# A hybrid decoder trunk on one core: the residual is updated before it is multiplied by the next norm's weights

## The chip, the core and the metric

One Trainium2 chip, of which the kernel uses one core. Its engines are PE (TensorE, matmuls; PEld is its weight load), DVE (VectorE), ACT (ScalarE), POOL (GpSimd) and SP (which here only issues transfers). They run side by side and meet through semaphores. The metric is the device time of one execution in microseconds (us); less is better.

## The reference, cut to what matters

Two layers over 256 tokens of width 1024. Each layer has two "sandwich" norms: the output of a block is normalised and added to the residual x, and x is normalised again before the next block.

```python
def _rms_norm(x, g):
    y = x * rsqrt(mean(x * x, axis=-1) + 1e-6)
    return y * g
...
for l in range(DEPTH):
    h = _rms_norm(x, g_pre_mix[l])
    ...                                    # h @ w_in, eight NSA heads, eight forgetting heads
    mix = concatenate([o_nsa, o_fox]) @ w_out[l]
    x = x + _rms_norm(mix, g_post_mix[l])
    h = _rms_norm(x, g_pre_mlp[l])
    y = square(relu(h @ w_up[l])) @ w_down[l]
    x = x + _rms_norm(y, g_post_mlp[l])
```

The row factor rsqrt(mean(x*x)) of a pre-norm commutes with the matmul behind it, so the kernel feeds the matmul with x times g_pre alone and applies the factor later. What a norm boundary must deliver to PE is therefore (x + r * acc * g_post) * g_pre, transposed, where acc is the block's output and r its row factor. There are three such boundaries: layer 0 attention to MLP, layer 0 MLP to layer 1, layer 1 attention to MLP. The last norm of all only updates x and stores it.

## The kernel before, in words

The 256 tokens are two tiles t = 0, 1 of 128 rows; `X[t]` holds the residual (128x1024, fp32, in SBUF). Every large product is made of three fp32r matmuls: an operand is split into a rounded part and a rest (`whi`, `wlo` for weights, two halves of `xT` for activations), ACT writes the rounded part and DVE the rest. In the profile `x<-whi,xT` is a matmul that writes the PSUM tile `x` from these two. PSUM tiles are called `x`, `acc`, `s`, `o` after their pools; the residual reads as `x` as well.

A block's output stands in four PSUM banks, two 512-column halves n = 0, 1 for each token tile: pool `x` for t = 0 and pool `acc` for t = 1 after attention and after the MLP. `sandwich` makes one boundary for one token tile: ACT squares both halves (`rl`, `sq`), `rsqrt_sum` makes r from them in a few one-column instructions on DVE and ACT (`rsqrt`), DVE makes the operand of the next block, `to_xT` transposes it on PE half by half (four 128x128 transposes against the identity `cst` into a bank `s`), and `split` copies the bank into `xT` (ACT the rounded part, then DVE the rest). The next block's first products for t = 0 read `xT` of t = 0 (bank `s` in the MLP, bank `o` in layer 1), those of t = 1 that of t = 1. A product over k = 0..3 needs the columns of half n = 0 only, one over k = 4..7 those of n = 1.

Before the change `pre_gain` prepares, ahead of a boundary, `xo[t]` = X[t] * g_next (two 128x1024 products) and the product of both weights, g_next * g_post. `sandwich` then reads acc once for `mg` = acc * (g_next * g_post), and makes the operand as mg * r + xo in four pieces of 256 columns. Only later, in its last part, it reads acc a second time for `m` = acc * g_post, and updates X[t] with m * r + X[t].

What order the instructions have: the kernel is recorded first (`Recorder`), every operation with an engine, a cost and its dependencies. `schedule` then plays the recorded operations through a list scheduler; on each engine the ready operation of lowest rank goes next, those marked urgent (`nc.hot`, here the steps of `sandwich` up to the transposes) ahead of all others. The order that comes out is fixed in the program: each engine issues its instructions in it. Since every operation is issued by one helper line, all of them carry the line L454 in the profile, and are told apart by their tiles. `RANKS` overrides the ranks of some twenty operations by hand, by their number in the recording. `ENTER` and `LEAVE` are costs that the scheduler adds where PE goes from full 128x128 matmuls to ones that use a part of the array, or back.

Of the kernel before, what the change touches and what calls it, by code (L numbers as in the profile page):

```python
# [18 lines left out]
F32 = mybir.dt.float32  # L19
F32R = mybir.dt.float32r  # L20
AF = mybir.ActivationFunctionType
OP = mybir.AluOpType
PSUM = bass.MemoryType.PSUM

P = 128
D = 1024
S = 256
NT = 2
# [13 lines left out]
RAMP = {0: 900, 1: 420}  # L42
WAIT = 0.7
WARM = (256, 256, 256, 256, 128)
ENTER, LEAVE = 90, 200
SEQ = [(2, 0), (2, 1), (2, 2), (2, 3), (3, 0), (3, 1), (3, 2), (3, 3)]
EVKEY = 1
FIRSTS = [(k, k + 1) for k in range(8)]
# [7 lines left out]
            "pr", "prT", "x0", "x1", "fV", "hs", "cs", "pcT", "vbig", "vS", "vW", "kstk", "kstv", "rT")  # L56
PAIRS = ("NSSSSSSSSSSSSN", "NSSSSSSSSSSSSS")
RANKS = (
# [4 lines left out]
)  # L63
EPS = 1e-6

# [133 lines left out]
class Recorder:  # L199
# [134 lines left out]
    def schedule(self):  # L334
# [10 lines left out]
        busy = dict.fromkeys(waiting, 0.0)  # L345
        bus, tiled, loads = 0.0, (P, P), 0
# [29 lines left out]
        while events:  # L376
            t, _, released = heapq.heappop(events)
# [4 lines left out]
            for e, ops in waiting.items():  # L382
                while busy[e] <= t:
                    best = None
                    for op in ops:
                        if op.ready <= t and (best is None or (best.urgent, -best.rank) < (op.urgent, -op.rank)) and fits(op):
                            best = op
                    if best is None:
                        break
                    if e == "tensor" and best.small and not small_last and not best.urgent and t < best.ready + HOLD:  # L390
                        more = [op for op in ops if op.ready <= t and fits(op)]
                        if sum(op.small for op in more) < 2:
                            best = min((op for op in more if not op.small), key=lambda op: op.rank, default=best)
                    if e == "tensor" and small_last and not best.urgent and not best.small:
                        more = [op for op in ops if op.small and op.ready <= t and op.rank < best.rank + REACH and fits(op)]
                        best = min(more, key=lambda op: op.rank, default=best)
# [15 lines left out]
                    if e == "sync":  # L412
                        busy[e] = t + 450
                        bus = max(bus, t + 1150) + best.cost + RAMP.get(loads, 0)
                        best.end = bus + 900 + (LATE if loads >= len(FIRSTS) else 0)
                        loads += 1
                    elif best.name == "dma_start":
                        busy[e] = t + 1000
                        bus = max(bus, t + 1150) + ADDING
                        best.end = bus + ADDED  # L420
                    else:
                        busy[e] = best.end = t + best.cost
                        small_last = best.small if e == "tensor" else small_last
                        if e == "tensor" and best.tile != tiled:
                            busy[e] = best.end = best.end + (tiled == (P, P)) * ENTER + (tiled != (P, P)) * LEAVE
                            tiled = best.tile
                    count += 1
                    heapq.heappush(events, (busy[e], count, None))
# [188 lines left out]
def trunk(nc, A, consts_in, out, sbp, pp, dram):  # L617
    def tile(shape, dtype, name, tag=None, bufs=1):
        return nc.tile(sbp[(tag or name) not in OPERANDS], shape, dtype, name, tag, bufs)
# [23 lines left out]
    for l in range(DEPTH):  # L643
# [34 lines left out]
        n = len(PAIRS[l])  # L678
# [15 lines left out]
    X = [tile([P, D], F32, name=f"x{t}") for t in range(NT)]  # L694
# [111 lines left out]

    def pre_gain(g_post, g_next):

        xo = []
        for t in range(NT):  # L810
            xo.append(tile([P, D], F32, name="xo", tag="fT", bufs=2))
            nc.vector.tensor_mul(xo[t], X[t], g_next)
        nc.vector.tensor_mul(g_next, g_next, g_post)
        return g_next, xo

    def sandwich(t, acc, g_post, pre=None, xT=None, eps=EPS, store=None):


        sq = small([P, 2], "sq")
        m, mg = [None, None], [None, None]  # L820

        def times(name, n, gain):
            y = tokt(name)
            nc.vector.tensor_mul(y, acc[n], gain[:, half(n)])
            return y

        for n in range(2):
            junk = small([P, 512], "rl")
            nc.scalar.activation(junk, acc[n], AF.Square, scale=1.0 / 32.0, accum_out=sq[:, n:n + 1])
            if pre:  # L830
                mg[n] = times("mg", n, pre[0])
            if n == 0 and not pre:
                m[0] = times("m", 0, g_post)
        r = rsqrt_sum(sq[:, 0:1], sq[:, 1:2], eps, store is not None)
        if not pre:
            m[1] = times("m", 1, g_post)
        if pre:
            xg = []
            for n in range(2):
                xg.append(mg[n])  # L840
                for c in (0, 256):
                    a = n * 512 + c
                    nc.vector.scalar_tensor_tensor(xg[n][:, c:c + 256], mg[n][:, c:c + 256], r,
                                                   pre[1][t][:, a:a + 256], op0=OP.mult, op1=OP.add)
            yield
            for n in range(2):
                to_xT(t, n, xg[n], xT)
            yield
        for n in range(2):
            if pre:  # L850
                m[n] = times("m", n, g_post)
            nc.vector.scalar_tensor_tensor(X[t][:, half(n)], m[n], r, X[t][:, half(n)],
                                           op0=OP.mult, op1=OP.add)
            if store is not None:
                nc.sync.dma_start(store[:, half(n)], X[t][:, half(n)])
        yield
# [982 lines left out]
```

## Time and profile before

| | before |
|---|---|
| median of 3 runs | 600.65 us (600.21 to 600.78) |
| the profiled execution | 600.97 us, of which the span of its instructions is 599.2 us |
| granted TensorE clock | 0.999 |
| instructions | PE 3323, DVE 1201, ACT 896, POOL 52 |
| chain that ended last | PE 96%, DMA 1%, DVE 1% of the span |

The span runs from the first to the last instruction of the profiled execution. Rows of a timeline read: start in us from the span's start, length in us, engine, line, operation, names out<-in, shapes, count. Lengths of neighbouring rows on one engine overlap: a 128x512 matmul is shown 0.39 us long while the next starts earlier, so the distance between starts is what counts on PE.

### The profile page before, as it was taken

To read this page: it belongs to the slowest core of one execution; us is meant where nothing else is said; L and a number is where in the kernel's file an instruction comes from. 1 tells how busy PE (TensorE), PEld (TensorE's weight loads), DVE (VectorE), ACT (ScalarE), POOL (GpSimd) and SP (SyncE) were. 2 spreads that over 40 slices of the span, in tenths; PEclk is the share of its full clock that TensorE was granted. 3 is DMA by queue.
4 is the path that set the end of the run, shared out by engine and by line. 5 is a ranking of instruction groups with operands and counts; after the bars stand their busy time and mean duration, and the time that the engine had idled before them with its cause. 6 is when DMAs were issued, how large, how long until landed. Compare 5 with 4: busy or idle time off the path is not lost.

```text
span 599.2 us, 9915 instructions
## 1 busy us (share of the span) xinstructions
PE 591.8 (99%) x3323; PEld 495.3 (83%) x3323; DVE 556.1 (93%) x1201; ACT 490.7 (82%) x896; POOL 35.9 (6%) x52
## 2 busy tenths in 40 slices
PE   9999999999999999999999999999999999999995
PEld 7988887788888888888888888777888888888884
DVE  7899999989999999999798999988999999999975
ACT  7678788677999999998667859875889999999973
POOL 0000200001010101010000020000110100101000
PEclk9999999999999999999999999999999999999999
DMA  8996729639889888989347762684598888888621
GB/s 320 385 341 204 260 80 308 206 112 277 291 243 285 234 256 251 271 248 296 107 142 263 262 243 75 194 265 141 135 311 233 271 236 262 250 253 264 173 36 71
DMA packets 39427, 135.64 MB, mean 226 GB/s; under 512 B 4656, under 2 KB 4816, under 8 KB 39376
## 3 DMA queue, kind: packets, MB, share of 16 engines
q1 hardware_dynamic: 34768, 118.23, 57.1%
q0 software_dynamic: 4608, 16.78, 15.9%
q8 instruction: 26, 0.43, 0.3%
q14 instruction: 25, 0.20, 0.1%
HBM read 133.92 MB, written 1.07 MB: 225 GB/s over the span
## 4 chain that ended last, share of the span: by engine, by line
PE 96%; DMA 1%; DVE 1%; ACT 0%; issue 0%; DVEq 0%
PE s L454 41%; PE acc L454 25%; PE x L454 21%; PE o L454 10%; DMA wraw<-in_w_out_dram 1%; DVE pr L454 0%; DVE wlo L454 0%; ACT whi L454 0%; DVE pcs L454 0%; DVE gz L454 0%; DVE x L454 0%; DVE m L454 0%; DVEq L1835 0%; DVE fkT L454 0%; DVE rsqrt L454 0%
## 5 line engine op out<-in xcount | busy, mean ns | idle before, releaser
L454 ACT ACTIVATE whi<-wraw 128x1024 fp32r<-128x1024 f32 (+2 forms) x188 | 181.3, 980 | 18.9 <-PE acc L454 7.4
L454 DVE TENSOR_TENSOR wlo<-wraw,whi 128x1024 fp32r<-128x1024 f32 (+1 forms) x156 | 171.5, 1108 | 5.6 <-ACT whi L454 4.7
L454 PE MATMUL s<-xT,whi 128*128 128x512 f32 x448 | 111.1, 390 | 0.0
L454 PEld LDWEIGHTS s<-xT,whi 128*128 128x128 f32 x448 | 83.9, 188 | 17.5
L454 PEld LDWEIGHTS s<-xT,wlo 128*128 128x128 f32 x448 | 61.1, 191 | 4.7 <-DMA wlo<-in_w_up_dram 0.4
L454 PE MATMUL s<-xT,wlo 128*128 128x256 f32 x448 | 62.6, 283 | 0.0
L454 DVE TENSOR_TENSOR wlo<-wsum,whi 128x1024 fp32r<-128x1024 f32 x50 | 61.0, 1220 | 1.5 <-ACT whi L454 1.2
L454 ACT ACTIVATE whi<-wsum 128x1024 fp32r<-128x1024 f32 x50 | 52.8, 1056 | 8.1 <-PE s L454 7.4
L454 POOL DMA_DIRECT2D wlo<-in_w_up_dram x32 | 27.8, 870 | 388.3 <-ACT wlo L454 225.0
L454 PE MATMUL x<-whi,aS 128*128 128x512 f32 x124 | 47.8, 391 | 0.0
L454 ACT ACTIVATE pr<-pr,st 128x256 f32<-128x256 f32 (+1 forms) x96 | 42.7, 448 | 4.8 <-DVE st L454 4.8
L454 PE MATMUL acc<-whi,aS 128*128 128x512 f32 x124 | 44.6, 392 | 0.0
L454 ACT ACTIVATE y<-s 128x512 f32<-128x512 f32 x56 | 32.7, 583 | 5.5 <-PE s L454 5.2
L454 PE MATMUL x<-whi,xT 128*128 128x512 f32 x112 | 35.8, 400 | 0.0
L454 PE MATMUL s<-whi,aS 128*128 128x512 f32 x100 | 35.4, 392 | 0.0
L454 PE MATMUL acc<-xT,whi 128*128 128x512 f32 x128 | 35.0, 399 | 0.0
L454 DVE TENSOR_TENSOR wsum<-wraw,wsum 128x512 f32<-128x512 f32 x50 | 34.3, 687 | 0.5
L454 PE MATMUL acc<-whi,xT 128*128 128x512 f32 (+1 forms) x128 | 34.7, 346 | 0.0
L454 ACT ACTIVATE wlo<-wraw 128x1024 fp32r<-128x1024 f32 x32 | 33.5, 1047 | 1.2 <-PE o L454 1.1
L454 DVE TENSOR_TENSOR aS<-quads,aS 128x896 fp32r<-128x896 f32 (+3 forms) x30 | 30.3, 1011 | 0.6 <-ACT aS L454 0.6
L454 DVE TENSOR_TENSOR wsum<-wraw 128x1024 f32<-128x1024 f32 x25 | 30.5, 1219 | 0.0
L454 ACT ACTIVATE aS<-quads 128x896 fp32r<-128x896 f32 (+3 forms) x30 | 26.5, 885 | 3.0 <-DVE quads L454 2.6
(256 smaller groups left out, 1275.9 us busy)
## 6 DMA issues: line engine op xcount, KB each, us to landing
wraw<-in_w_up_dram SPq DMA_DIRECT2D x64, 512.0 KB, 5.0
wraw<-in_w_down_dram SPq DMA_DIRECT2D x64, 512.0 KB, 5.9
wraw<-in_w_in_dram SPq DMA_DIRECT2D x36, 512.0 KB, 4.8
wlo<-in_w_up_dram POOLq DMA_DIRECT2D x32, 512.0 KB, 7.5
wraw<-in_w_out_dram SPq DMA_DIRECT2D x16, 512.0 KB, 4.4
w<-in_cmp_w_k_dram SPq DMA_DIRECT2D x8, 512.0 KB, 4.0
w<-in_cmp_w_v_dram SPq DMA_DIRECT2D x8, 512.0 KB, 4.9
bias<-sums SPq DMA_DIRECT2D x8, 384.0 KB, 7.8
```

The costliest lines, as they stand in the source:

```text
L454: getattr(getattr(self.nc, op.engine), name)(*[real(v) for v in args], **{k: real(v) for k, v in kw.items()})
```

## The change

`pre_gain` does nothing any more but hand on g_next. In `sandwich` acc is read once, for m = acc * g_post; X[t] is updated in place in four pieces of 256 columns, and each piece is multiplied by g_next, into the place of m, to be transposed. So `xo`, the product of the two weights, the second reading of acc and the update of X in halves of 512 columns are gone, and a product of 128x256, both operands in SBUF, is new for each piece. The last norm (pre is None) is as it was. The scheduler gets a third cost, `TURN`, for going from one part-array form to another, and `RANKS` other entries; both only move instructions.

```diff
-ENTER, LEAVE = 90, 200
+ENTER, LEAVE, TURN = 90, 200, 95
 RANKS = (
-    (613, 64655.99960082749), (1021, 87750.99950762419), (1109, 100388), (1161, 109377), (1199, 97914),
...
+    (734, 74971), (767, 80709), (870, 86842), (1062, 90308), (1101, 103698), (1230, 118019), (1293, 109200),
...
-                            busy[e] = best.end = best.end + (tiled == (P, P)) * ENTER + (tiled != (P, P)) * LEAVE
+                            busy[e] = best.end = best.end + (
+                                ENTER if tiled == (P, P) else LEAVE if best.tile == (P, P) else TURN)
...
     def pre_gain(g_post, g_next):
 
-        xo = []
-        for t in range(NT):
-            xo.append(tile([P, D], F32, name="xo", tag="fT", bufs=2))
-            nc.vector.tensor_mul(xo[t], X[t], g_next)
-        nc.vector.tensor_mul(g_next, g_next, g_post)
-        return g_next, xo
+        return g_next
...
-            if pre:
-                mg[n] = times("mg", n, pre[0])
-            if n == 0 and not pre:
-                m[0] = times("m", 0, g_post)
+            if n == 0 or pre is not None:
+                m[n] = times("m", n, g_post)
...
-        if pre:
+        if pre is not None:
             xg = []
             for n in range(2):
-                xg.append(mg[n])
+                xg.append(m[n])
                 for c in (0, 256):
-                    a = n * 512 + c
-                    nc.vector.scalar_tensor_tensor(xg[n][:, c:c + 256], mg[n][:, c:c + 256], r,
-                                                   pre[1][t][:, a:a + 256], op0=OP.mult, op1=OP.add)
+                    y, x = m[n][:, c:c + 256], X[t][:, n * 512 + c:n * 512 + c + 256]
+                    nc.vector.scalar_tensor_tensor(x, y, r, x, op0=OP.mult, op1=OP.add)
+                    nc.vector.tensor_mul(y, x, pre[:, n * 512 + c:n * 512 + c + 256])
...
-        for n in range(2):
-            if pre:
-                m[n] = times("m", n, g_post)
+        for n in range(2 * (pre is None)):
             nc.vector.scalar_tensor_tensor(X[t][:, half(n)], m[n], r, X[t][:, half(n)],
                                            op0=OP.mult, op1=OP.add)
```

Both programs have the same matmuls in number and shape. Up to some 57 us of the trace their order is the same; behind that the scheduler puts them otherwise nearly everywhere. The three boundaries are shown here.

First boundary (layer 0, attention to MLP), DVE. Before, from the first products of acc for t = 0 to the copies of the transposed tile (`xT`); `rsqrt` is the row factor:

```order
L454 TENSOR_TENSOR mg<-x,gains 128x512
L454 TENSOR_SCALAR rsqrt<-sq,rsqrt 128x1
L454 SCALAR_TENSOR_TENSOR rsqrt<-rsqrt 128x1 x2
L454 SCALAR_TENSOR_TENSOR mg<-mg,rsqrt,xo 128x256 x4
L454 TENSOR_SCALAR rsqrt<-sq 128x1
L454 TENSOR_TENSOR mg<-acc,gains 128x512
L454 TENSOR_SCALAR rsqrt<-rsqrt 128x1
L454 TENSOR_TENSOR xT<-s,xT 128x4x128 x2
```

Now, at the same place; `x_778` is the residual X[0] in SBUF:

```order
L454 TENSOR_SCALAR rsqrt<-sq,rsqrt 128x1
L454 TENSOR_TENSOR m<-x,gains 128x512
L454 SCALAR_TENSOR_TENSOR rsqrt<-rsqrt 128x1 x2
L454 SCALAR_TENSOR_TENSOR x_778<-m,rsqrt,x_778 128x256 x3
L454 TENSOR_TENSOR m<-x_778,gains 128x256 x2
L454 TENSOR_SCALAR rsqrt<-sq 128x1
L454 TENSOR_TENSOR m<-acc,gains 128x512
L454 SCALAR_TENSOR_TENSOR x_778<-m,rsqrt,x_778 128x256
L454 TENSOR_TENSOR m<-x_778,gains 128x256 x2
L454 TENSOR_TENSOR xT<-s,xT 128x4x128
```

The operand of half n = 0 is ready after three updates and two products instead of two updates, and the operand of n = 1 stands behind a product of t = 1 besides.

The same boundary on PE, t = 0. The transposes read `s<-cst,mg` before and `s<-cst,m` now; `acc<-whi,oT` and `acc<-wlo,oT` are the last products of the attention block for t = 1, and `s<-whi,xT` the first of the MLP. Before:

```order
L454 MATMUL acc<-whi,oT 128x512 x2
L454 MATMUL s<-cst,mg 128x128 x4
L454 MATMUL acc<-wlo,oT 128x512
L454 MATMUL s<-cst,mg 128x128 x4
L454 MATMUL acc<-whi,oT 128x512 x2
L454 MATMUL acc<-wlo,oT 128x512
L454 MATMUL acc<-whi,oT 128x512 x2
L454 MATMUL acc<-wlo,oT 128x512
L454 MATMUL acc<-whi,oT 128x512
L454 MATMUL s<-whi,xT 128x512
```

Now:

```order
L454 MATMUL acc<-wlo,oT 128x512
L454 MATMUL s<-cst,m 128x128 x4
L454 MATMUL acc<-whi,oT 128x512 x2
L454 MATMUL acc<-wlo,oT 128x512
L454 MATMUL acc<-whi,oT 128x512
L454 MATMUL s<-cst,m 128x128 x4
L454 MATMUL s<-whi,xT 128x512
```

Of the 24 matmuls for t = 1, 16 stood ahead of the first transposes, one between the two groups and seven behind; now 20 stand ahead, four between, and none behind. Somewhat later, for t = 1, the transposes stood in one group of eight, with six matmuls of bank `s` behind them ahead of the first that reads the new tile (`o<-whi,xT`). There stands now:

```order
L454 MATMUL s<-cst,m 128x128 x4
L454 MATMUL s<-whi,xT 128x512 x2
L454 MATMUL o<-whi,xT 128x512
L454 MATMUL s<-cst,m 128x128 x4
L454 MATMUL o<-wlo,xT 128x512
```

so that two matmuls separate the first four transposes from the first reader of their tile.

Second boundary (layer 0 MLP to layer 1), PE, t = 0; `o<-whi,xT` is the first product of layer 1, `acc<-whi,aT` the last of the MLP. Before:

```order
L454 MATMUL s<-cst,mg 128x128 x4
L454 MATMUL acc<-wlo,aT 128x512
L454 MATMUL acc<-whi,aT 128x512
L454 MATMUL s<-cst,mg 128x128 x4
L454 MATMUL acc<-whi,aT 128x512
L454 MATMUL acc<-wlo,aT 128x512
L454 MATMUL acc<-whi,aT 128x512
L454 MATMUL o<-whi,xT 128x512
```

Now:

```order
L454 MATMUL s<-cst,m 128x128 x4
L454 MATMUL acc<-wlo,aT 128x512
L454 MATMUL acc<-whi,aT 128x512
L454 MATMUL o<-whi,xT 128x512
L454 MATMUL o<-wlo,xT 128x512
L454 MATMUL acc<-whi,xT 128x288
L454 MATMUL o<-whi,xT 128x512 x2
L454 MATMUL o<-wlo,xT 128x512
L454 MATMUL s<-cst,m 128x128 x4
```

Two matmuls instead of nine matmuls and transposes now stand between the first group of transposes and `o<-whi,xT`. For t = 1 four matmuls stand there now (`o<-whi,xT`, `o<-wlo,xT`, `o<-whi,xT` and then `x<-whi,xT`, which is the reader).

Third boundary (layer 1, attention to MLP), DVE, t = 0, now (before it was as at the first boundary):

```order
L454 SCALAR_TENSOR_TENSOR x_778<-m,rsqrt,x_778 128x256 x2
L454 TENSOR_TENSOR m<-x_778,gains 128x256 x2
L454 TENSOR_SCALAR rsqrt<-sq 128x1
L454 TENSOR_TENSOR m<-acc,gains 128x512
L454 SCALAR_TENSOR_TENSOR x_778<-m,rsqrt,x_778 128x256 x2
L454 TENSOR_TENSOR m<-x_778,gains 128x256
L454 TENSOR_TENSOR xT<-s,xT 128x4x128
L454 TENSOR_TENSOR m<-x_778,gains 128x256
L454 TENSOR_TENSOR m<-acc,gains 128x512
```

The copy `xT<-s,xT` of half n = 0 stands ahead of the last piece of n = 1. PE has the same order there as at the first boundary: four transposes, four matmuls of `acc`, four transposes, then `s<-whi,xT`.

More of the change, by code (lines that the diff above doesn't have):

```diff
@@ L829, in sandwich @@
             nc.scalar.activation(junk, acc[n], AF.Square, scale=1.0 / 32.0, accum_out=sq[:, n:n + 1])
-            if pre:
-                mg[n] = times("mg", n, pre[0])
-            if n == 0 and not pre:
-                m[0] = times("m", 0, g_post)
+            if n == 0 or pre is not None:
+                m[n] = times("m", n, g_post)
         r = rsqrt_sum(sq[:, 0:1], sq[:, 1:2], eps, store is not None)
-        if not pre:
+        if pre is None:
             m[1] = times("m", 1, g_post)
-        if pre:
+        if pre is not None:
             xg = []
             for n in range(2):
-                xg.append(mg[n])
+                xg.append(m[n])
                 for c in (0, 256):
-                    a = n * 512 + c
-                    nc.vector.scalar_tensor_tensor(xg[n][:, c:c + 256], mg[n][:, c:c + 256], r,
-                                                   pre[1][t][:, a:a + 256], op0=OP.mult, op1=OP.add)
+                    y, x = m[n][:, c:c + 256], X[t][:, n * 512 + c:n * 512 + c + 256]
+                    nc.vector.scalar_tensor_tensor(x, y, r, x, op0=OP.mult, op1=OP.add)
+                    nc.vector.tensor_mul(y, x, pre[:, n * 512 + c:n * 512 + c + 256])
             yield
```

5 rows, old and new, of the table RANKS are left out of this document.

## The prediction, made before the changed kernel was run

> **What bounds the kernel now.** I read the shares of the engines first, then who waits for whom on PE, then the three boundaries in time.
>
> ```profile
> PE   591.8 (99%) x3323; PEld 495.3 (83%) x3323; DVE 556.1 (93%) x1201; ACT 490.7 (82%) x896; POOL 35.9 (6%) x52
> ```
>
> PE is busy for 99% of the span, DVE for 93%. A busy share alone doesn't say that PE binds, since the ends of matmuls are modelled and overlap, so I look at waits and at distances between starts. The waits of PE and of its weight load (waited for, us, times, longest), with the two largest that name an engine:
>
> ```profile
> PE o L454 <- PEq L1829: 0.8, 1, 0.8
> PEld s L454 <- ACT pr L454: 1.0, 3, 0.4
> PEld x L454 <- ACT xT L454: 0.5, 2, 0.3
> ```
>
> PE's only wait is the start of the program. Its weight load waits a little for ACT, but runs ahead of the matmuls, and none of it reaches PE's row. Now the boundaries, as stretches of 20 us (busy time of PE, PEld, DVE, ACT, POOL):
>
> ```profile
> core 0: us, PE busy (x) PEld busy (x) DVE busy (x) ACT busy (x) POOL busy (x), PEclk, DMA share, GB/s
> 120.00:140.00 20.00, 20.00 (x100) 16.68 (x99) 17.52 (x36) 14.53 (x27) 1.88 (x2) 1.00 0.52 150
> 291.00:311.00 20.00, 20.00 (x99) 16.55 (x98) 17.49 (x39) 11.31 (x26) 0.00 (x0) 1.00 0.35 106
> 414.00:434.00 20.00, 20.00 (x100) 16.71 (x99) 17.38 (x36) 14.39 (x26) 1.74 (x2) 1.00 0.51 134
> ```
>
> and from the chain that ended last, the sixteen matmuls ahead of the transposes at the first and at the third boundary:
>
> ```profile
> 122.80 3.63 PE acc L454 x16
> ...
> 416.95 3.63 PE acc L454 x16
> ```
>
> 3.63 / 16 = 0.227 us from start to start, with full clock. So PE runs without a gap through all three boundaries, and what DVE does there (17.5 of 20 us) is hidden. Two things follow. Work taken from DVE there buys nothing, because PE has no wait to lose. And any new wait of PE is paid in full: PE is as full before and behind, and makes nothing up.
>
> **The work on DVE.** These are the groups that the change touches (count, busy us and mean ns of one); the last row stands for the new product, same shape and both operands in SBUF:
>
> ```profile
> L454 DVE TENSOR_TENSOR xo<-x,gains 128x1024 f32<-128x1024 f32 x6 | 7.2, 1214 | 0.2 <-PE s L454 0.2
> L454 DVE TENSOR_TENSOR gains<-gains 128x1024 f32<-128x1024 f32 x3 | 3.7, 1217 | 0.0
> L454 DVE TENSOR_TENSOR m<-acc,gains 128x512 f32<-128x512 f32 x8 | 5.4, 685 | 0.6 <-ACT rl L454 0.6
> L454 DVE SCALAR_TENSOR_TENSOR x<-m,rsqrt,x 128x512 f32<-128x512 f32 x16 | 11.6, 746 | 0.1
> L454 DVE SCALAR_TENSOR_TENSOR mg<-mg,rsqrt,xo 128x256 f32<-128x256 f32 x24 | 10.0, 480 | 0.2
> L454 DVE TENSOR_TENSOR quads<-quads 128x256 f32<-128x256 f32 x28 | 11.6, 419 | 0.0
> ```
>
> For one boundary there go two `xo` (2 x 1.214), the product of the weights (1.217), four second products (4 x 0.685) and four updates (4 x 0.746): 9.37 us. The eight pieces of 256 stay, with X as their target, and eight products of 0.419 come: 3.35. That is 6.0 us less per boundary, 18 us of DVE's 556, nine instructions fewer. The cover that makes it worth nothing is PE itself, as shown. `xo` and the second products lay off the path; the new products lie on it, between r and the transposes. The buffers of `xo` and the banks of acc come free earlier, and so do the loads of the next norm weights, which SP issues between weight transfers: nothing on PE waited for either before, so I put both at zero; if SP's queue were late, PE would show it as a wait on a weight transfer.
>
> **What the longer chain costs PE.** First the pace of the steps, at the first boundary:
>
> ```profile
> 122.64 0.39 PE L454 MATMUL acc<-whi,oT 128*128 128x512 f32 x1
> 124.17 0.20 DVE L454 TENSOR_SCALAR rsqrt<-sq,rsqrt 128x1 f32<-128x1 f32 x1
> 126.27 0.60 PE L454 MATMUL s<-cst,mg 128*128 128x128 f32 x4
> 126.63 0.48 PE L454 MATMUL acc<-wlo,oT 128*128 128x512 f32 x1
> 126.95 0.60 PE L454 MATMUL s<-cst,mg 128*128 128x128 f32 x4
> ...
> 130.15 0.21 DVE L454 TENSOR_SCALAR rsqrt<-sq,rsqrt 128x1 f32<-128x1 f32 x1
> 130.28 0.68 DVE L454 TENSOR_TENSOR mg<-acc,gains 128x512 f32<-128x512 f32 x1
> 130.87 0.41 DVE L454 SCALAR_TENSOR_TENSOR rsqrt<-rsqrt 128x1 f32<-128x1 f32 x2
> 131.31 1.67 DVE L454 SCALAR_TENSOR_TENSOR mg<-mg,rsqrt,xo 128x256 f32<-128x256 f32 x4
> 133.09 1.04 PE L454 MATMUL s<-cst,mg 128*128 128x128 f32 x8
> 133.73 1.09 ACT L454 ACTIVATE xT<-s 128x512 fp32r<-128x512 f32 x2 [0.43 <-PE s L454]
> 134.36 0.69 DVE L454 TENSOR_TENSOR xT<-s,xT 128x512 fp32r<-128x512 f32 x1 [0.24 <-ACT xT L454]
> ...
> 145.23 0.76 DVE L454 TENSOR_TENSOR quads<-quads 128x256 f32<-128x256 f32 x2
> ...
> 290.58 0.64 ACT L454 ACTIVATE aT<-h 128x512 fp32r<-128x512 f32 x1
> 291.27 0.19 PEld L454 LDWEIGHTS x<-whi,aT 128*128 128x128 f32 x1 [0.15 <-ACT aT L454]
> 291.38 0.40 PE L454 MATMUL x<-whi,aT 128*128 128x512 f32 x1
> ```
>
> On PE: if four transposes start at T, the next matmul starts at T+0.36 (126.27 to 126.63), the one behind it 0.32 later (to 126.95), each further one 0.23 later. From transposes to the reader: ACT copies from T+0.64 (133.09 to 133.73), DVE makes the rest from T+1.27 (134.36), 0.69 long. The two copies by ACT take 1.09, so one has ended at about T+0.64+0.59. A weight load starts 0.05 behind the end of an ACT row (291.22 to 291.27), its matmul 0.11 later: the first reader of the rounded part starts at T+1.39 at the earliest. On DVE: a piece of 256 takes 0.40 to the next start (1.67 for four, the last shown 0.48 long), a new product 0.34 (0.76 less 0.42), a product of 512 0.59 (130.28 to 130.87), the root's last steps 0.44 (130.87 to 131.31). Now the places.
>
> First boundary, t = 0. DVE starts the root's step at 124.17 as before; m follows 0.13 later at 124.30, the root at 124.89, three updates from 125.33, two products at 126.53 and 126.87, ended at 127.29. PE reaches the transposes after 20 matmuls at 122.64 + 20 x 0.227 = 127.18, the third of them at 127.40; it can start at 127.29 + 0.16 = 127.45: 0.05 lost. For half n = 1 DVE goes on with a step (0.13), m of t = 1 (0.59), an update (0.40) and two products, ended at 129.09, so the third transpose can start at 129.25. PE, with four matmuls between, is there at 128.80. Lost: 0.45, with the first 0.50.
>
> First boundary, t = 1. Two matmuls stand between the transposes and the first reader: PE is there at T+0.36+0.32+0.23 = T+0.91, the tile at T+1.39. Lost: 0.48.
>
> Second boundary. For t = 0 again two matmuls: 0.48. The matmul with the rest of xT comes 0.59 after that first reader (two of 0.23, one of 288 columns of about 0.13), at T+1.98, and the rest is there at T+1.27+0.69+0.16 = T+2.12: 0.14. For t = 1 the reader is fourth: T+1.14 against T+1.39, 0.25.
>
> Third boundary, t = 0. The last product of n = 1 stands behind `xT<-s,xT` on DVE's queue, which can't start ahead of T+1.27; it follows at T+1.87 (0.60 for 512 columns) and ends at T+2.29, its transpose starts at T+2.45. PE is there at T+0.36+0.32+3 x 0.23 + 0.22 = T+1.59. Lost: 0.86. What waits behind these transposes is all of PE. For t = 1 the order leaves enough matmuls between.
>
> Sum: 0.50 + 0.48 + 0.48 + 0.14 + 0.25 + 0.86 = 2.7 us. Counted in the two orders, PE changes its array form 38 times instead of 36. The trace doesn't price one change alone; it is bounded by nothing below (it may be hidden) and by a gap between two starts above, 0.23 each; I take 0.1 each, so 0.2. Everywhere else the order is rebuilt too. PE has no wait to lose there; new ones can't be read off the order. I bound them by 0 and by 1.5, the two weight-load waits quoted come through in full, and take 0, since before not one did. Against the profiled execution that is 600.97 + 2.9 = 603.9; the median of the runs is 0.3 below it, so I predict **603.6 us**.
>
> [...] The trace shows four pieces in 1.67 us where four lengths of 0.48 make 1.92, so starts overlap the ends here. By full lengths the stretch between the two pairs of products would be some 0.4 us longer, and the time about 604.0; I keep the starts.
>
> **The rivals.** (1) No change: the waits above come, but the order elsewhere gives them back, or PE finds them smaller because a copy is quicker than its row. For it: the cost of each place rests on some 0.1 us steps, and a scheduler that lost 2.7 us at one place could win at others. Against it: there is nothing to win but gaps on PE, and there are none. With half of each loss, and no price for the forms, it gives 600.65 + 1.35 = 602.0, just over the border of what can be told; with three quarters gone 601.3, which is the time I give it.
>
> (2) Faster: DVE binds, not PE. At 93% it is the fullest engine beside PE, and 18 us of work go. If DVE set the time in the boundaries, those 6.0 us each would come off: 582.6 at the most. [...] It would decide from the point where PE's starts stand apart by more than 0.227 ahead of the transposes. They don't, by the rows above, so it gets little.
>
> (3) Slower by more: at the second boundary the conversion of a weight tile (1.2 us) stands between the last steps of the root for t = 1, and the rebuilt attention stage may bring waits of its own. With the 1.5 of above it gives 605.1.
>
> **How the numbers follow.** 0.2% (1.2 us) is about what a measurement of this kernel can tell from no change. My forecast (601.9 to 605.0): 0.64; rival 1: 0.25; rival 2: 0.06; rival 3: 0.05. So slower 0.69, same 0.25, faster 0.06. The range reaches from 600.5, which takes in most of rival 1, to 605.1; the forecast's own is 601.9 to 605.0.
>
> **What would show it.** PE's row should have idle time at the boundaries, some 0.5 us ended by ACT's `xT` at the first and the second, and 0.4 to 0.9 us ended by DVE's `m` ahead of the transposes at the first and the third; the stretches of 20 us should read 19 to 19.7 us of PE. DVE should have 1192 instructions and some 538 us, without `xo` and `mg`. The sixteen-matmul runs elsewhere should keep 3.63. It is wrong if PE reads 20.00 in those stretches, or if gaps of that size come up in the attention or MLP stages.

## The result, and the profile after

The changed kernel takes 607.78 us (median of 4 executions, 607.10 to 609.86), the kernel before 600.71 beside it: 1.012 times as long (95% interval 1.011 to 1.0138). I had forecast 603.6 us (600.5 to 605.1). The sign was right; the loss, 7.1 us, is more than twice the 2.9 us forecast.

The profiled execution is the slowest of the four, 609.86 us with a span of 608.1 (the others have spans of 605.3, 605.5 and 606.5). Its busy times, and the chain that ended last:

```profile
PE 596.1 (98%) x3323; PEld 494.6 (81%) x3323; DVE 542.2 (89%) x1192; ACT 491.8 (81%) x896; POOL 36.1 (6%) x52
...
PE 88%; DMA 4%; ACT 3%; DVE 2%; issue 1%; DVEq 0%; POOLq 0%; ACTq 0%
```

DVE has nine instructions and 14 us less than before, and the program is longer: PE's share of the chain fell from 96% to 88%. Whom PE now waits for (us in total, times, longest):

```profile
PE s L454 <- ACT y L454: 1.1, 1, 1.1
PE x L454 <- DVE qS L454: 1.0, 1, 1.0
PE s L454 <- DMA wlo<-in_w_up_dram: 0.8, 1, 0.8
PE o L454 <- PEq L1820: 0.8, 1, 0.8
PE o L454 <- ACT xT L454: 0.5, 2, 0.3
PE o L454 <- ACT aS L454: 0.5, 1, 0.5
PE s L454 <- DVE m L454: 0.5, 1, 0.5
PE x L454 <- DVE gcol L454: 0.2, 1, 0.2
```

Before, the start of the program (`PEq`) was the only such row; the 0.2 us for `gcol` lie in its first 5 us too. Two of the new ones belong to the norms, `ACT xT` and `DVE m`, 1.0 us together. The larger ones do not: `y` and `aS` are made in layer 0's MLP, `qS` in layer 1's attention, the transfer `wlo<-in_w_up_dram` feeds layer 1's MLP. The same in stretches (length, then busy PE, PEld, DVE, ACT, POOL, the granted clock, DMA): first the three of the prediction, then these three.

```profile
120.00:140.00 20.00, 19.78 (x96) 16.10 (x95) 18.63 (x41) 13.46 (x25) 1.01 (x1) 1.00 0.28 91
291.00:311.00 20.00, 19.71 (x93) 15.74 (x91) 17.55 (x40) 13.65 (x31) 0.00 (x0) 1.00 0.35 106
414.00:434.00 20.00, 19.52 (x100) 15.30 (x99) 15.23 (x32) 11.23 (x23) 0.00 (x0) 1.00 0.22 71
155.00:175.00 20.00, 18.40 (x88) 15.22 (x87) 17.12 (x29) 18.03 (x30) 1.37 (x2) 0.91 0.94 305
335.00:350.00 15.00, 13.99 (x103) 10.79 (x102) 11.54 (x30) 10.02 (x17) 0.00 (x0) 1.00 0.72 246
530.00:545.00 15.00, 14.21 (x75) 11.90 (x74) 13.74 (x21) 12.79 (x18) 0.86 (x1) 1.00 0.98 264
```

Between 155 and 175 us the granted clock is 0.91 as well. Cut finer, that is one interval of 3.41 us at half clock, right behind the idle time:

```profile
161.94:165.35 3.41, 1.81 (x9) 1.05 (x7) 3.41 (x6) 3.41 (x8) 0.00 (x0) 1.00 0.91 366
165.35:168.76 3.41, 3.41 (x11) 2.73 (x10) 3.15 (x7) 2.51 (x5) 0.86 (x1) 0.50 0.65 160
```

To size each place I took all distances between starts of neighbouring matmuls and subtracted the usual one (0.227 us for 512 columns, 0.120 for 256, 0.110 for a transpose). This excess is 9.0 us larger than before in the profiled execution, whose span is 8.9 us longer:

| place | excess over the kernel before, us |
|---|---|
| the three norms (122 to 136, 292 to 312, 415 to 436) | 2.3 |
| layer 0's MLP, 162 to 169 (1.27 + 0.67 of waiting, 0.2 in the next distances, 1.6 of half clock) | 3.7 |
| layer 1's attention, 343 to 347 | 1.35 |
| layer 1's MLP, 538 | 0.95 |
| all other places | 0.7 |

So the norms cost what the prediction had put there, and more than twice as much is lost some 25 to 110 us behind them. The half clock is in this execution's time; whether the other three had it, no trace shows. Two theories can hold. A: the longer chain at the norms makes the whole loss; where it comes to light says nothing. B: the chain costs about 2 us, and the other 5 belong to the order that the scheduler and its table made of the new recording.

### The profile page after: what moved, and what is told of

The parts are those of the page before. It is cut to its first block, busy times and chain, and to the rows that moved or that the text cites. A ratio compares the mean times of both kernels' runs of the same rounds, so it can differ in the third digit from the quotient of the medians.

```text
span 608.1 us, 9909 instructions
## 1 busy us (share of the span) xinstructions
PE 596.1 (98%) x3323; PEld 494.6 (81%) x3323; DVE 542.2 (89%) x1192; ACT 491.8 (81%) x896; POOL 36.1 (6%) x52
## 4 chain that ended last, share of the span: by engine, by line
PE 88%; DMA 4%; ACT 3%; DVE 2%; issue 1%; DVEq 0%; POOLq 0%; ACTq 0%
PE s L454 38%; PE acc L454 22%; PE x L454 18%; PE o L454 9%; DMA wlo<-in_w_up_dram 2%; ACT whi L454 1%; DMA wraw<-in_w_out_dram 1%; DMA wraw<-in_w_in_dram 1%; DMA first<-in_first_dram 1%; DVE m L454 1%; ACT rl L454 0%; DVE x L454 0%; DVE wlo L454 0%; ACT kx L454 0%; ACT aS L454 0%
```

## The experiments

Most of these kernels replace the scheduler by a written list, which fixes the order of every engine:

```diff
-        for i, rank in RANKS:
-            self.ops[i].rank = rank
-        return self.schedule()
+        return [self.ops[i] for i in PLAN]
```

Where instructions were "re-placed", the places come from trying moves against the scheduler's own costs; the times below are all measured. `before` was 600.3 to 600.7 us beside each of them.

**The new arithmetic in the old order.** `PLAN` is the order of before with the removed instructions left out.

> The changed arithmetic, with every other instruction in the place it had before the change: the two added products stand right behind the updates they belong to, the removed instructions are left out, and nothing else moves on any engine. Theory A (the loss of 7.1 us is the longer chain at the three norms, wherever it stands): the same 607.8 us as the changed kernel. Theory B (the chain costs about 2 us where the order around it gives way, as the boundaries of the changed kernel's trace show, and the other 5 us come from places in the MLP and in layer 1's attention that the rebuilt order made late): the gaps at 162, 343 and 538 us must be gone; but here nothing gives way at the norms. From rows of before, the first half of a token tile is ready 0.84 us later and the second 1.67 us later (two more 256-column instructions of 0.42 us a half), for two token tiles at three norms, less what stood free: between 3 x 2 x 0.9 = 5.4 and 3 x 2 x 1.67 = 10 us, all of it in gaps ahead of the transposes of m: 606 to 610.7 us, and no gap over 0.4 us elsewhere.

608.33 us (607.68 to 608.70). The median alone looks like theory A, but the losses have moved. PE's waits, without the start's:

```profile
PE s L454 <- DVE m L454: 3.1, 9, 0.5
PE s L454 <- DVE rsqrt L454: 0.7, 2, 0.4
PE o L454 <- DVE xT L454: 0.3, 1, 0.3
PE s L454 <- DMA wlo<-in_w_up_dram: 0.3, 1, 0.3
```

`y`, `aS` and `qS` are gone, nine waits for `m` have come. The excess at the three norms is 7.6 us over before, and the kernel is 7.7 us slower. With nothing moved out of its way the chain costs 7.7 us; the changed kernel's order brought that down to 2.3 and lost the difference again elsewhere.

**The same, eased at the norms only.** Within some 25 us around each norm instructions are re-placed, above all the transposes of m. PE at the first norm, t = 0, in the kernel above (-) and now (+):

```
-L454 MATMUL s<-cst,m 128x128 x4
 L454 MATMUL acc<-wlo,oT 128x512
-L454 MATMUL s<-cst,m 128x128 x4
+L454 MATMUL s<-cst,m 128x128 x4
 L454 MATMUL acc<-whi,oT 128x512 x2
 L454 MATMUL acc<-wlo,oT 128x512
 L454 MATMUL acc<-whi,oT 128x512 x2
 L454 MATMUL acc<-wlo,oT 128x512
 L454 MATMUL acc<-whi,oT 128x512
+L454 MATMUL s<-cst,m 128x128 x4
 L454 MATMUL s<-whi,xT 128x512
```

So the first group stands one matmul later, the second seven.

> As the kernel with the changed arithmetic in the old order, but around the three norms (stretches of about 25 us) instructions are re-placed so that the transposes of m stand a few matmuls later on TensorE. Everywhere else the order is that of before. Theory A: no place near the norms hides the chain, so about 607 us. Theory B: what is left is the boundaries' own loss, which the changed kernel's trace puts at 2.0 us and the prediction put at 2.7: 602.5 to 603.5 us, with the gaps at 162, 343 and 538 us and the half-clock stretch behind 165 us all absent.

602.46 us (601.80 to 602.97; ratio 1.0029, interval 1.0018 to 1.0041), 1.8 us over before. In its trace the same matmuls take 1.8 us longer around the three norms than before. Its waits:

```profile
PE s L454 <- DMA wlo<-in_w_up_dram: 0.8, 1, 0.8
PE o L454 <- PEq L1820: 0.8, 1, 0.8
PE s L454 <- ACT quads L454: 0.5, 1, 0.5
PE s L454 <- DVE m L454: 0.2, 1, 0.2
```

That decides for B: the same arithmetic is 5.3 us faster than the changed kernel, in another order. The waits for `y`, `aS` and `qS` are absent; the one for the transfer is not, and needs a look. At this place the transfers are issued as in the kernel before, to 0.01 us relative to each other, and yet took longer (KB, us from issue to landing; before first, then this kernel):

```profile
wraw<-in_w_up_dram SPq DMA_DIRECT2D x1, 512.0 KB, 3.7
wlo<-in_w_up_dram POOLq DMA_DIRECT2D x1, 512.0 KB, 8.4
wraw<-in_w_down_dram SPq DMA_DIRECT2D x1, 512.0 KB, 5.2
```

```profile
wraw<-in_w_up_dram SPq DMA_DIRECT2D x1, 512.0 KB, 3.9
wlo<-in_w_up_dram POOLq DMA_DIRECT2D x1, 512.0 KB, 10.2
wraw<-in_w_down_dram SPq DMA_DIRECT2D x1, 512.0 KB, 9.0
```

So a wait at this place can come in the old order too. How often differs, though: in the eight traces of this document with the old order there, before among them, this transfer took 8.3 to 8.5 us five times, and PE did not wait, and 9.6, 9.6 and 10.2 us, and PE waited 0.3, 0.3 and 0.8 us; in the four with the changed order it took 9.9 or 10.0 us, and PE waited 0.7 or 0.8 us each time. Why the same transfers take longer in one execution than in another stays open.

**Eased in another way.**

> Like the kernel in the old order that was eased at the norms (602.46 us), with another placement around the three norms: the transposes of m, and the products and conversions near them, stand so that each has about 0.1 us more to spare. In that kernel's trace 0.48 us are lost at 298.5 (transposes of m waiting for the product by the next gains), 0.66 us at 439 (transposes of h, behind the third norm) and 0.15 us at 134; the 0.99 us at 541 us are a transfer that takes 8.4 to 10.2 us at the same place of the same order, so they may come or not. If the norms' own cost can be hidden by order alone, 601.0 to 601.8 us; if the chain costs its 2 us wherever the transposes stand, 602.3 to 603.5 us. Theory A is already out by the run before; it would say 607.

602.74 us (602.00 to 603.36): no better than 602.46. The waits for `m` are gone and waits for `xT` have taken their place (0.8 us, two times, and 0.2). Two unlike placements cost 1.8 and 2.4 us; that the chain of 256-column pieces costs about 2 us in any order is likely from this, but a better placement is not excluded.

**The changed kernel, mended in layer 0's MLP.** There PE waits for ACT, which works through its queue without a pause: `y`, which frees the bank that PE needs next, stands behind the squares `rl<-x` of the new residual.

```profile
162.09 0.61 ACT L454 ACTIVATE rl<-x 128x512 f32<-128x512 f32 x1
162.61 0.19 ACT L454 ACTIVATION_READ_ACCUMULATOR rl<-x 128x1 f32 x1
162.70 0.57 ACT L454 ACTIVATE y<-s 128x512 f32<-128x512 f32 x1
163.18 0.62 ACT L454 ACTIVATE rl<-x 128x512 f32<-128x512 f32 x1
163.33 0.19 PEld L454 LDWEIGHTS s<-whi,aS 128*128 128x128 f32 x1 [1.31 <-ACT y L454]
```

The edit moves, among others, `y` and `aS` ahead of these squares.

> The changed kernel with its own order, except that 39 instructions between 134 and 170 us (end of the second norm, start of layer 0's MLP) are re-placed, so that TensorE has other products to do while the rows of s and aS it lacked at 162 and 164 us are made. Theory A: 607.8 us, since these gaps are only where the chain's lateness comes out, and closing them moves it on. Theory B: of 1.27 + 0.67 us of gaps some 1.3 us go; and if the half clock of 165.3 to 168.7 us (0.51 granted, about 1.5 us) is a consequence of these gaps, it goes as well where it came: 604.5 to 606.5 us.

606.17 us (605.61 to 607.72), 1.6 us less. One gap of 1.11 us is left at 161 us, the second gap and the half clock are gone. In two later traces with the changed order at this place both gaps stand as before, and without the half clock the excess is 2.2 us there; here it is 1.25. So by the traces the edit itself is worth 0.9 us, and the half clock, where it comes, 1.6 more.

**Two instructions moved in layer 1's attention.** Here the head of ACT's queue waits for a transfer, and work that is ready stands behind it:

```profile
341.27 1.06 ACT L454 ACTIVATE whi<-wraw 128x1024 fp32r<-128x1024 f32 x1 [4.76 <-DMA wraw<-in_w_in_dram]
341.80 1.55 PE L454 MATMUL acc<-xT,whi 128*128 128x512 f32 x6
342.24 1.05 ACT L454 ACTIVATE qS<-s 64x512 fp32r<-64x512 f32 x2
...
344.36 0.51 PE L454 MATMUL x<-kx,qS 128*128 128x512 f32 x1 [1.01 <-DVE qS L454]
```

> The changed kernel with two instructions moved by two places each, in layer 1's attention: on ScalarE the conversion whi<-wraw that starts at 341.27 us behind the two copies qS<-s that follow it, and on VectorE its partner wlo<-wraw,whi behind the two qS<-s,qS. In the changed kernel's trace that conversion waits 4.76 us for its transfer while the copies, whose rows TensorE has made at about 341.1 us, stand behind it, and TensorE then stands idle 1.18 us before x<-kx,qS at 343 us. If the order is the cause, the copies start some 0.9 us earlier and the gap shrinks to about 0.3 us: 606.9 us. If the lateness of the transfers is the cause and not the order, the buffer of wraw comes free later by the 1.3 us that VectorE's instruction moves, the next loads start later and the loss comes back within the next 10 us: 607.5 to 608.5 us.

606.71 us (606.41 to 607.32), 1.1 us less. `x<-kx,qS` no longer waits, but a wait of 0.54 us came back one step later:

```profile
339.40 1.05 ACT L454 ACTIVATE whi<-wraw 128x1024 fp32r<-128x1024 f32 x1
339.53 1.28 DVE L454 TENSOR_TENSOR qS<-s,qS 64x512 fp32r<-64x512 f32 x2 [2.66 <-ACT qS L454]
...
340.98 0.62 PE L454 MATMUL x<-kx,qS 128*128 128x512 f32 x2
...
344.47 0.63 PE L454 MATMUL s<-cst,q_tok 128*128 128x128 f32 x4 [0.54 <-DVE qS L454]
```

The time is that of the first theory, the trace nearer to the second. The 1.01 us that `x<-kx,qS` waited belong to one execution: the kernel mended in the MLP has the same order at this place, and PE's wait there is

```profile
PE x L454 <- DVE qS L454: 0.3, 1, 0.3
```

and so it is in the kernel with TURN undone, below. Over the same matmuls (338 to 348 us) the excess is 1.5 us in the changed kernel's trace, 0.8 and 0.9 in those two, and 0.8 here. So the two moves shifted the wait more than they took it out. The 1.1 us of the time are barely clear of noise (the interval of the ratio to before is 1.0086 to 1.0114 here and 1.011 to 1.0138 for the changed kernel), and the half clock in the MLP, which is in the changed kernel's trace and not in this one, can make as much. What the two moves are worth stays open.

**Is it the table, the cost TURN, or the scheduler?** Both kernels with `RANKS = ()`:

> The kernel before without its table RANKS of 22 hand-set places: the scheduler's own order, the old arithmetic. It is the partner of the next run; what is asked is the difference of the two. Theory T1 (the new table fits its order worse than the old one did its own, and that is where the 4 to 5 us away from the norms come from): without tables the two kernels differ by the norms' own 2 us alone. Theory T2 (the scheduler's rule itself, fed with the longer chain at the norms, re-deals the work behind them worse, and the table only repairs some of it): they differ by 5 us or more without the tables too. For this one alone no reading of the trace gives a number; taking the table away can only leave more late places, so 601 to 608 us.

> The changed kernel without its table RANKS of 21 places: the scheduler's own order with the new arithmetic and the new cost TURN. T1: 1.5 to 3 us above the kernel before without its table. T2: 5 us or more above it, and above 607.8 us.

604.26 us (603.95 to 605.74) and 610.77 us (609.87 to 611.47). They differ by 6.5 us, hardly less than with their tables: T1 is out. Each table repairs 3 to 4 us of what its own scheduler run left. Without the table PE waits in the kernel before too, 1.9 us for the transfer and 1.5 for `y`; in the changed kernel without its table the largest excesses come to 2.4 us at the norms and 5.5 behind them, ahead of `o<-whi,aS`, `s<-xT,whi` and twice `s<-cst,h`. Then `TURN = 200`, the old rule's price, and nothing else:

> The changed kernel with the scheduler's new cost TURN set back to 200, which is what the old rule charged for a change from one smaller array form to another. The arithmetic and the table stay those of the changed kernel, and the orders differ at a handful of places on TensorE and VectorE, all in the two attention stages. If TURN has a share in the 5 us away from the norms, this kernel is faster than 607.8 us by more than 1 us. If it has none, it lands within 1 us of 607.8 us (the changed kernel's own executions lie between 607.1 and 609.9), with the gaps at 128 to 134, 162, 303, 430 and 538 us as they were.

607.54 us (606.90 to 608.51): TURN has no share that these runs can tell. By the tiles' names its order differs from the changed kernel's in one matmul and one DVE instruction near 105 us, so this cost hardly touches the order here.

**Wider pieces at the norms.** If the length of DVE's chain sets the norms' 1.8 us, fewer and wider instructions must shorten it:

```diff
-                for c in (0, 256):
-                    y, x = m[n][:, c:c + 256], X[t][:, n * 512 + c:n * 512 + c + 256]
-                    nc.vector.scalar_tensor_tensor(x, y, r, x, op0=OP.mult, op1=OP.add)
-                    nc.vector.tensor_mul(y, x, pre[:, n * 512 + c:n * 512 + c + 256])
+                y, x = m[n], X[t][:, half(n)]
+                nc.vector.scalar_tensor_tensor(x, y, r, x, op0=OP.mult, op1=OP.add)
+                nc.vector.tensor_mul(y, x, pre[:, half(n)])
```

In the old order with nothing eased, the partner of the first experiment:

> The same pieces of 512 columns in the old order with nothing eased: the partner of the run that put the new arithmetic in the old order (608.33 us, 7.07 us of gaps ahead of the transposes at the norms). If the gaps are the chain's length, the second halves come 0.6 us earlier at six token tiles: some 3.6 us less, 604.7 us (603.7 to 606). If they are the number of dependent steps or the waits between engines, not the columns, 607 to 608.5 us.

605.00 us (604.75 to 605.54), 3.3 us less than with narrow pieces. PE and ACT have the same order in both; DVE differs at the pieces alone (at three of the six token tiles both wide updates stand ahead of both products). Eased at the norms:

> The new arithmetic with pieces of 512 columns at the norms instead of 256: one update of X and one product by the next gains for each half, 4 instructions for a token tile instead of 8, in the old order and eased at the norms as in the two runs before. The same sums are made. By the traces two 256-column instructions take 0.84 us and one of 512 columns 0.685, so the first half is ready after 1.37 us instead of 1.67 and the second after 2.74 instead of 3.34; before the change they took 0.84 and 1.67. Theory: what is left of the loss (1.8 us in the eased order) is the length of this chain, and 0.3 to 0.6 us less at six token tiles takes all of it away: 600.3 to 601.5 us. Rival: the loss hangs on the transposes having to wait for X at all, or is paid elsewhere by then: 602 to 603 us. Below 600.0 us neither expects it, as TensorE has no idle time left at the norms to win.

600.81 us (600.39 to 601.56, 11 executions), against 600.73 for the kernel before: ratio 1.0003, interval 0.9994 to 1.0012. Its busy times and the whole list of PE's waits:

```profile
PE 591.5 (99%) x3323; PEld 493.8 (82%) x3323; DVE 539.8 (90%) x1168; ACT 490.3 (82%) x896; POOL 36.0 (6%) x52
```

```profile
PE o L454 <- PEq L1820: 0.8, 1, 0.8
```

The new arithmetic costs nothing here that the time can tell (0.4 us at the norms by its trace). It gains nothing either, with 16 us less on DVE than before the change. The places around the norms are not those of the two eased kernels with narrow pieces, so what is gained on them, 1.7 and 1.9 us, belongs to pieces and places together; the pair in the old order shows the pieces' share alone. Under the scheduler alone, without a table:

> The new arithmetic with pieces of 512 columns under the scheduler's own order without its table: the partner of the changed kernel without its table (610.77 us) and of the kernel before without its table (604.26 us). If the scheduler deals the work behind the norms worse because the chain is longer, a chain 0.3 to 0.6 us shorter a token tile should take away more than its own 2 to 3.6 us or about as much: 606 to 608.5 us. If what comes behind the norms has nothing to do with the chain's length, it stays within 1.5 us of 610.77 us.

609.47 us (608.93 to 609.96), 1.3 us under the narrow pieces' 610.77 and still 5.2 over the kernel before without its table. The kernel before took 600.73 us beside this one and 600.33 beside the other two; taken against it, the gain is 1.7 us and 4.8 are left. So the length of the chain is at most a small part of what makes the scheduler deal the work worse.

**What an idle PE costs besides.** The half clock behind 165 us was tried in the kernel before, with copies added on ACT ahead of some evictions `y`:

```diff
+        idle = rec.tile(sb[False], [P, 384], F32, name="idle", tag="idle")
+        for _ in range(21):
+            rec.scalar.activation(idle, rec.cst[:, :384], AF.Copy)
```

> The kernel before, with 21 copies (384 columns, about 0.42 us each) added on ScalarE ahead of four evictions y in layer 0's MLP, 3, 4, 6 and 8 of them, so that TensorE stands idle once near 181, 197, 221 and 248 us, for about 1.0, 1.3, 2.3 and 3.2 us. Nothing of the result changes. If the half clock in the changed kernel came from an idle of 1.3 us, the granted clock drops here behind at least the three longer ones, each for about 3.4 us at a loss of some 1.5 us: 600.7 + 7.8 + 4.5 = 613 us. If idles of this size do not matter (the changed kernel had idles of 1.18 and 0.95 us at 343 and 538 us without a drop), the time is 600.7 + 7.8 = 608.5 us and the clock stays 1.00 behind all of them. If only the longest count, 610 to 611.5 us.

613.09 us (611.75 to 614.04). The clock dropped behind the longest idle alone (4.08 us, then 6.83 us of half clock), not behind 1.15, 1.58 and 2.73 us. That the time is the 613 us of the first theory is chance: the idles came out longer than planned, 9.5 us in all instead of 7.8, and the trace is that of the third. Then eight equal ones:

> The kernel before with 40 copies added on ScalarE, five ahead of each of eight evictions y in layer 0's MLP (near 182, 194, 205, 218, 230, 243, 254 and 267 us), so that TensorE stands idle about 2.2 us eight times. With four single idles only the longest, 4.08 us, was followed by half clock; 2.73, 1.58 and 1.15 us were not; in the changed kernel two idles of 1.27 and 0.67 us within 3.3 us were. If the drop needs an idle of about 3.4 us or more, none of the eight drops: 600.7 + 17.5 = 618 us and clock 0.998. If the drop hangs on how the idle falls into a fixed raster of some 3.4 us, some of the eight drop (each worth about 1.7 us): 620 to 630 us.

629.49 us in one execution, clock 0.981: six of the eight were followed by half clock for 3.41 us, two were not, so the first theory is out. All six intervals begin on one raster: 183.65 us and then 4, 8, 16, 24 and 28 times 3.413 us later. Two of the idles, each with the raster interval it fell into and the next one (columns as above):

```profile
180.24:183.65 3.41, 1.32 (x6) 0.77 (x5) 1.72 (x3) 3.28 (x7) 0.00 (x0) 1.00 1.03 265
183.65:187.06 3.41, 3.41 (x9) 2.62 (x8) 2.89 (x4) 2.53 (x4) 0.77 (x1) 0.50 0.46 186
221.20:224.61 3.41, 2.21 (x13) 1.60 (x12) 2.40 (x5) 3.28 (x6) 0.00 (x0) 1.00 1.02 318
224.61:228.02 3.41, 2.68 (x12) 2.18 (x13) 2.18 (x3) 2.97 (x5) 0.00 (x0) 1.00 0.59 238
```

The first idle, 2.1 us by these rows, lies whole in one interval, and the next runs at 0.50; the second, 1.9 us, is cut by the raster into 1.2 and 0.7 us, and the clock stays.

## Why the prediction was wrong, point by point

**PE binds, and DVE's relief is worth nothing: right.** The wide pieces in the eased order show it best: DVE 16 us less, PE's waits as before, the time as before. The rival in which DVE binds (582.6 us) is out. DVE's own figure was a little off, 542.2 us instead of 538, without consequence.

**The boundaries, 2.7 us: right as a sum, and in most places.** The trace of after shows 2.3. First boundary, t = 0: forecast 0.50, found none, because the root's step started at 123.59 us and not at 124.17. Before, the product `mg` stood ahead of it; in the new order it is the first, as the order shown above the prediction has it, and I had kept its old time. Before, then now:

```profile
123.56 0.69 DVE L454 TENSOR_TENSOR mg<-x,gains 128x512 f32<-128x512 f32 x1 [0.18 <-ACT rl L454]
```

```profile
123.59 0.21 DVE L454 TENSOR_SCALAR rsqrt<-sq,rsqrt 128x1 f32<-128x1 f32 x1
123.72 0.68 DVE L454 TENSOR_TENSOR m<-x,gains 128x512 f32<-128x512 f32 x1
```

For t = 1 forecast 0.48, found 0.39. Second boundary: forecast 0.48 + 0.14, found 0.45 and two distances 0.11 longer than usual; then 0.25 against 0.16. Third: 0.86 against 0.64, the wait for `m` in the middle of the transposes, as written. That this is about the price of the new arithmetic in pieces of 256 columns, whatever comes behind, is shown by the eased order: 1.8 us in the time. The 0.2 us for two more changes of array form no run prices.

**"Everywhere else in the rebuilt order", 0 to 1.5 us, taken as 0: the step that failed.** It measured about 5: the changed kernel's 607.78 less the 602.46 that the same arithmetic takes when only the norms are re-ordered. Its places are the waits for `y` and `aS` in layer 0's MLP (2.2 us, with the half clock 3.7), for `qS` in layer 1's attention and for the transfer in layer 1's MLP, which are the gaps in the attention and MLP stages that the prediction named as a sign of being wrong. Mending the first took 1.6 us out of the time, and its trace agrees; with the two moves at the second the time fell by 1.1, but their trace shows the wait moved more than gone. I had seen that the scheduler puts the instructions otherwise nearly everywhere behind 57 us, and still priced this at nothing, on the grounds that PE had no wait in the old order. But a PE without waits is a property of one order, not of the program: without its table the kernel before takes 604.26 us, and PE waits for `y` and for the transfer there too. The upper end of 1.5 was two waits of the weight load in the old order (1.0 and 0.5 us); they say nothing of what a new order brings, and the range inherited that.

**The queues, put at zero: half right.** The sign to watch for, a wait of PE on a weight transfer, did come (0.8 us at 538 us, and 0.7 in each of the three other traces with this order there); in the unchanged order it comes in some executions only. The loads of the next norm's weights nowhere end a wait of PE.

**The rival "slower by more" (605.1 us)** had the right place in part: new waits in attention came (1.35 us in this execution, less in others), the one between the root's steps at the second boundary did not. It fell short because it did not count the MLP, or the half clock that came behind PE's idle time there (1.6 us in the profiled execution).

**What stays open:** why the scheduler deals the work behind the norms worse with the new recording. Not for TURN and not for its table; narrow or wide pieces matter 1.3 us out of 6.5 (1.7 against the kernel before beside each). How much of the 5 us each place is worth is known only in part, since the waits at 343 and 538 us vary between executions. What is left is that `xo`, the second products and the late updates are missing, and that the squares of X are ready earlier; neither was tried by itself.

## What to carry to other kernels

When a change re-deals the order of a kernel whose bound engine has no gap left, price the order first: put the new instructions into the old order, everything else fixed, and ease it only where they stand. That separates what the arithmetic costs (here 1.8 us, and 0.1 with wider pieces) from what the new order costs (5 us). And on a dependent chain count instructions, not only columns: cutting a half into two pieces whose transposes stand in one group made the chain longer, and the kernel in the old order 3.3 us slower (608.33 us against 605.00).

## What the runs showed of the hardware

Two narrow DVE instructions took longer here than one wide one: in the trace of after an update or product of 256 columns is 0.481 or 0.420 us long, in the wide version one of 512 columns 0.749 or 0.686.

```profile
L454 DVE SCALAR_TENSOR_TENSOR x<-m,rsqrt,x 128x256 f32<-128x256 f32 x24 | 10.6, 481 | 0.2
L454 DVE TENSOR_TENSOR m<-x,gains 128x256 f32<-128x256 f32 x24 | 9.2, 420 | 0.0
```

```profile
L454 DVE TENSOR_TENSOR m<-x,gains 128x512 f32<-128x512 f32 x20 | 13.6, 686 | 4.9 <-ACT rl L454 4.8
L454 DVE SCALAR_TENSOR_TENSOR x<-m,rsqrt,x 128x512 f32<-128x512 f32 x16 | 11.7, 749 | 0.3
```

By these lengths a cut costs 2 x 0.420 - 0.686 = 0.15 us for a product and 0.21 for an update. The lengths reach over the next start, though. From start to start, where the next instruction does not need the result, a narrow update takes 0.40 us and a narrow product 0.34 in the changed kernel, a wide one 0.67 and 0.60 in the eased wide one; by that a cut costs 0.13 us for an update and 0.07 for a product. A product right behind the update that it needs starts 0.51 us behind it, not 0.40: so in all 24 pairs of the new arithmetic in the old order. The 3.3 us that the wide pieces bring in the old order (608.33 us to 605.00) point the same way.

The changes of TensorE's granted clock lie on a raster of 3.413 us in these traces. In the changed kernel's it falls to half at 165.35 us, is full again from 168.76, and falls to half once more at 605.67, behind the last matmul: 3.41 us and then 436.91, which is 128 times 3.4133. Counted back in such steps, the first line of the raster lies 1.51 us behind the start of the span there, 0.08 in the trace of before (half clock from 597.41 us on, behind the last matmul) and 2.74 in the run with eight idles (from 183.65 us). For every raster interval of the changed kernel and of the two with idles, up to the last matmul, I summed the time that no matmul covers, each matmul counted with its usual distance. In nine intervals this was 2.05 to 2.52 us, and behind each of them the next ran at half clock; in all others it was 2.02 us or less, and none followed. In the traces of the other kernels none comes over 1.9 us, and the clock stays full up to there. That is a count over these traces; what sets the granted clock they do not show. In the changed kernel the two gaps of 1.27 and 0.67 us fell into one interval in the profiled execution (2.15 us in all) and 3.41 us of half clock followed. The same two gaps are in the profiled executions of the kernel with two instructions moved and of that with TURN undone, where a line of the raster lies between them, and the clock stayed full (0.999 over the execution in both, against 0.995). The 1.6 us that this costs can so come and go with the execution, which can be part of why the changed kernel's executions spread over 2.8 us; only one of the four was traced.
